# Low parts of the last six rows of W_out: two Pool operations in the place of one VectorE operation

## The chip, the core and the metric

The kernel runs on one core of a Trainium2 chip. The core has five engines, each with an instruction queue of its own that is worked off in order: TensorE (PE in the profile; PEld is its weight load), VectorE (DVE), ScalarE (ACT), GpSimd (POOL) and SyncE (SP, which here issues every DMA). The metric is the device time of one execution in microseconds; less is better.

## What is computed

One layer of a hybrid decoder. The input is normalised and projected, three groups of heads (a linear recurrence, a dilated-window attention and a state-space group, "SSD") make 2048 mixed columns, and these go through one output projection:

```python
mix = jnp.concatenate([y_lru, y_attn, y_ssd], axis=-1) @ w_out
out = x + rmsnorm(mix, post_g)
```

`w_out` is 2048 x 1024. The prompt has 2048 tokens. The products keep float32 accuracy: each operand is split into a high part in the rounded type fp32r and a low part, the difference, and three products of the four are summed.

## The kernel before

The program is written with a tile framework that sets the order of the instructions on each engine when the program is built. It takes the author's order as a guide and places an instruction where it reckons its operands to be ready, so a change of engine in one line moves neighbours too. On the chip the order is then fixed.

The stages are: projection (to about 1,110 us), sample tokens, prompt attention (to about 1,420 us), and a last stage in which two things run interleaved. One is the SSD group, 16 chunks of 128 tokens, each in two halves `g`; in it DVE, ACT and Pool make decay matrices (`sg`), scaled inputs (`xdt`, `xte`), the state (`hT`) and a group norm (`sq`, `rs`, `rB`), and PE makes the products `yd`, `yo` and `stp`. The other is `out_chunk`, the output projection: for each chunk of 128 tokens two output halves (`hf`, 512 columns each, tile `ops`), each a sum over 16 rows k of `W_out` blocks of three matmuls (`mm3`, lines 82 to 84: high by high, high by low, low by high). Rows 0 to 7 take `mh` and `ml`, the two other groups' output; rows 8 to 15 take `sh` and `sl`, the SSD group's. `ops` tiles lie in a pool of three.

`W_out` comes in just ahead of its first use. Rows 0 to 9 (`load_wo_slab`) are loaded whole in the attention stage. Rows 10 to 15 (`load_wo_rest`) are loaded in halves of 512 columns into a tile `wr` under the tag "x" that has two buffers, one for each half. For each half line 1001 makes the high part on ACT (`wo10h` to `wo15h`) and line 1002 the low part on DVE (`wo10l` to `wo15l`). Line 1002 is the last reader of `wr`; the DMA of the same half of the next row (line 1018) waits for it. The rows' scale is 1 for k below 8, and a column of the group-norm weight (`ngc`) for the others.

So the rows 10 to 15 go round a loop: DMA into `wr`, high part, low part, DMA of the next row. It lies in the first chunk of `out_chunk`, from about 1,436 to 1,465 us. Beside it the order puts matmuls of chunk 1's first output half.

Of the kernel before, what the change touches and what calls it, by code (L numbers as in the profile page):

```python
# [8 lines left out]
F32 = mybir.dt.float32  # L9
F32R = mybir.dt.float32r  # L10
AF = mybir.ActivationFunctionType
OP = mybir.AluOpType
# [15 lines left out]
W_SLAB = 10  # L28
# [4 lines left out]
def tile_hybrid_step(ctx: ExitStack, tc: tile.TileContext, A):  # L33
    nc = tc.nc
    act, dve, pool, pe, sp = nc.scalar, nc.vector, nc.gpsimd, nc.tensor, nc.sync
# [84 lines left out]
    def big(name, n=1024, dt=F32R):  # L120

        if n > 1024:
            return slab.tile([128, n], dt, tag="C", name=name, bufs=8)
        return slab.tile([128, n], dt, tag="A", name=name)
# [320 lines left out]
    with tc.tile_pool(name="dtp", bufs=1) as dp:  # L445
# [6 lines left out]
                                 op0=OP.mult, op1=OP.mult)  # L452
# [542 lines left out]
    wo = {}  # L995

    def load_wo(k, raw):
        wo[k] = [big(f"wo{k}{c}", 1024 if k < 12 else XC)[:, :DM] for c in "hl"]
        sc_ = 1.0 if k < 8 else ngc[:, k - 8:k - 7]
        for r, sl in raw:  # L1000
            act.activation(out=wo[k][0][:, sl], in_=r, func=AF.Copy, scale=sc_)
            dve.scalar_tensor_tensor(out=wo[k][1][:, sl], in0=r, scalar=sc_, in1=wo[k][0][:, sl].bitcast(F32),
                                     op0=OP.mult, op1=OP.subtract)

    def load_wo_slab():
        for k in range(W_SLAB):
            raw = big("wraw", dt=F32)
            sp.dma_start(out=raw, in_=A["w_out"][0, 128 * k:128 * k + 128])
            yield
            load_wo(k, [(raw, slice(0, DM))])  # L1010
            yield

    def load_wo_rest(pl):
        for k in range(W_SLAB, 16):
            raw = []
            for sl in (slice(0, 512), slice(512, DM)):
                raw.append((pl.tile([128, 512], F32, tag="x", name="wr", bufs=2), sl))
                sp.dma_start(out=raw[-1][0], in_=A["w_out"][0, 128 * k:128 * k + 128, sl])
            load_wo(k, raw)
            yield  # L1020
# [501 lines left out]
    for c in range(16):  # L1522
        k = 0
# [115 lines left out]
```

## Time and profile before

| | us |
|---|---|
| median of three runs | 1939.15 (1937.5 to 1939.77) |
| profiled execution, its own time | 1935.46 |
| its span in the trace | 1933.7 |
| PE busy in the span | 1888.0 (98%) |
| DVE busy | 1075.8 (56%) |
| ACT busy | 760.3 (39%) |
| POOL busy | 269.4 (14%) |

The profile is that of one execution. The span is what lies between its first and last instruction. Busy PE is modelled: a matmul's end is its result's arrival, so consecutive matmuls overlap in the rows, and an idle time before a matmul is the stretch in which none was under way.

### The profile page before, as it was taken

To read this page: it belongs to the slowest core of one execution; us is meant where nothing else is said; L and a number is where in the kernel's file an instruction comes from. 1 tells how busy PE (TensorE), PEld (TensorE's weight loads), DVE (VectorE), ACT (ScalarE), POOL (GpSimd) and SP (SyncE) were. 2 spreads that over 40 slices of the span, in tenths; PEclk is the share of its full clock that TensorE was granted. 3 is DMA by queue.
4 is the path that set the end of the run, shared out by engine and by line. 5 is a ranking of instruction groups with operands and counts; after the bars stand their busy time and mean duration, and the time that the engine had idled before them with its cause. 6 is when DMAs were issued, how large, how long until landed. Compare 5 with 4: busy or idle time off the path is not lost.

```text
span 1933.7 us, 35729 instructions
## 1 busy us (share of the span) xinstructions
PE 1888.0 (98%) x14110; PEld 1552.6 (80%) x14110; DVE 1075.8 (56%) x2354; ACT 760.3 (39%) x1490; POOL 269.4 (14%) x346
## 2 busy tenths in 40 slices
PE   8999999999999999999999999999998999999998
PEld 7998888888888888887877777777766787677876
DVE  7414444454533776664422226666687776667774
ACT  6411636362610222223233436555654333333332
POOL 0100111101010111111000100000023223223231
PEclk9999999999999999998999999999999999999999
DMA  7422121232233222224477753343465444334442
GB/s 235 131 79 74 44 69 47 64 69 63 66 88 79 94 76 74 67 72 138 131 210 205 208 181 115 101 142 102 119 207 161 127 140 124 111 115 130 128 140 66
DMA packets 304500, 222.02 MB, mean 115 GB/s; under 512 B 69171, under 2 KB 260515, under 8 KB 304333
## 3 DMA queue, kind: packets, MB, share of 16 engines
q1 hardware_dynamic: 304332, 219.74, 38.7%
q8 instruction: 111, 1.82, 0.4%
q14 instruction: 57, 0.46, 0.1%
HBM read 150.81 MB, written 68.86 MB: 114 GB/s over the span
## 4 chain that ended last, share of the span: by engine, by line
PE 41%; ACT 4%; DMA 3%; DVE 3%; issue 1%; SPq 1%; POOL 1%; DVEq 0%; ACTq 0%; POOLq 0%
PE ops L83 5%; PE ops L84 5%; PE ops L82 5%; PE mm L82 3%; PE pt L1164 3%; PE mm L84 3%; PE mm L83 3%; PE o L1200 2%; ACT sr L1136 2%; PE s L1109 2%; PE yd L1283 2%; DMA sg<-d_cum 1%; PE yo L1288 1%; PE s L1088 1%; PE stp L1307 1%
## 5 line engine op out<-in xcount | busy, mean ns | idle before, releaser
L82 PE MATMUL mm<-xh,wh 128*128 128x512 f32 (+2 forms) x1600 | 562.4, 351 | 1.8 <-ACT wh L147 0.9
L83 PE MATMUL mm<-xl,wh 128*128 128x512 f32 (+2 forms) x1600 | 561.2, 351 | 0.0
L84 PE MATMUL mm<-xh,wl 128*128 128x512 f32 (+2 forms) x1600 | 559.9, 350 | 0.0
L82 PEld LDWEIGHTS mm<-xh,wh 128*128 128x128 f32 x1600 | 301.5, 188 | 44.4 <-issue 4.3
L84 PEld LDWEIGHTS mm<-xh,wl 128*128 128x128 f32 x1600 | 300.6, 188 | 39.6 <-issue 1.0
L83 PEld LDWEIGHTS mm<-xl,wh 128*128 128x128 f32 x1600 | 301.2, 188 | 37.7 <-issue 0.2
L146 POOL TENSOR_TENSOR wr<-wr,gC 128x1024 f32<-128x1024 f32 x40 | 78.7, 1968 | 407.6 <-DMA wr<-in_w_in_dram 379.5
L436 DVE SCALAR_TENSOR_TENSOR o<-u,ssdc,o 128x512 f32<-128x512 f32 (+2 forms) x216 | 128.6, 618 | 4.8
L1136 ACT ACTIVATE sr<-sr,nm 128x384 f32<-128x384 f32 (+3 forms) x128 | 97.9, 770 | 23.3 <-DVE nm L1132 18.7
L148 DVE SCALAR_TENSOR_TENSOR wl<-wr,wh 128x1024 fp32r<-128x1024 f32 x40 | 48.9, 1223 | 82.9 <-ACT wh L147 82.9
L642 ACT ACTIVATE o<-o 128x512 f32<-128x512 f32 (+2 forms) x60 | 33.1, 552 | 145.7 <-issue 83.2
L1047 ACT COPY ptsb<-pt 128x512 f32<-128x512 f32 x96 | 52.5, 583 | 76.7 <-PE pt L1164 76.6
L720 DVE TENSOR_SCALAR sg<-sg,cum 128x128 f32<-128x128 f32 (+1 forms) x256 | 72.8, 344 | 14.7 <-ACT ecB L718 14.6
L82 PE MATMUL mmt<-wh,xh 128*128 128x256 f32 (+3 forms) x272 | 79.5, 295 | 0.9 <-ACT xh L254 0.6
L84 PE MATMUL mmt<-wh,xl 128*128 128x256 f32 (+3 forms) x272 | 78.6, 290 | 0.0
L83 PE MATMUL mmt<-wl,xh 128*128 128x256 f32 (+3 forms) x272 | 78.1, 288 | 0.0
L434 DVE TENSOR_SCALAR o<-u,ssdc 128x512 f32<-128x512 f32 (+1 forms) x72 | 43.1, 611 | 61.9 <-ACT u L416 60.7
L1164 PE MATMUL pt<-ident,sr 128*128 128x128 f32 x576 | 75.3, 281 | 2.3 <-ACT sr L1136 1.8
L147 ACT ACTIVATE wh<-wr 128x1024 fp32r<-128x1024 f32 x40 | 42.4, 1060 | 87.9 <-PE mm L83 76.9
L1164 PEld LDWEIGHTS pt<-ident,sr 128*128 128x128 f32 x576 | 63.6, 143 | 15.0 <-issue 8.9
L416 ACT COPY u<-mm 128x512 f32<-128x512 f32 (+1 forms) x80 | 39.4, 493 | 91.9 <-PE mm L84 80.2
L718 ACT ACTIVATE ecB<-sg 64x512 f32<-64x512 f32 x60 | 37.8, 630 | 88.3 <-DMA sg<-d_cum 80.5
(520 smaller groups left out, 3551.3 us busy)
## 6 DMA issues: line engine op xcount, KB each, us to landing
wr<-in_w_in_dram SPq DMA_DIRECT2D x40, 512.0 KB
sg<-d_cum SPq DMA_DIRECT2D x30, 512.0 KB
d_xbc<-o SPq DMA_DIRECT2D x36, 256.0 KB
x<-in_x_prompt_dram SPq DMA_DIRECT2D x32, 256.0 KB
kc<-in_cache_attn_k_dram SPq DMA_DIRECT2D x32, 256.0 KB
vt<-in_cache_attn_v_dram SPq DMA_DIRECT2D x32, 256.0 KB
xres<-in_x_prompt_dram SPq DMA_DIRECT2D x32, 256.0 KB
out_dram<-ot SPq DMA_DIRECT2D x32, 256.0 KB
```

What stands on the lines that cost most here:

```text
L82: pe.matmul(out, lhsT=wh, rhs=xh, start=start, stop=False)
L83: pe.matmul(out, lhsT=wh, rhs=xl, start=False, stop=False)
L84: pe.matmul(out, lhsT=wl, rhs=xh, start=False, stop=stop)
L146: pool.tensor_tensor(out=wr, in0=wr, in1=gC[:, :, None].to_broadcast([128, 8, 128]), op=OP.mult)
L147: act.activation(out=wh, in_=wr, func=AF.Copy, scale=scale)
L148: dve.scalar_tensor_tensor(out=wl, in0=wr, scalar=scale, in1=wh.bitcast(F32), op0=OP.mult, op1=OP.subtract)
L434: dve.tensor_scalar(out=o, in0=v(0), scalar1=w[:, 0:1], scalar2=b, op0=OP.mult, op1=OP.add)
L436: dve.scalar_tensor_tensor(out=o, in0=v(t), scalar=w[:, t:t + 1], in1=o, op0=OP.mult, op1=OP.add)
L720: dve.tensor_scalar(out=sg[:n, h], in0=sg[:n, h], scalar1=cum[:n, c, 8 * g + h:8 * g + h + 1], scalar2=0.0, op0=OP.subtract, op1=OP.min)
L1047: act.copy(out=out, in_=in_)
L1136: act.activation(out=sr[e][r], in_=sr[e][r], func=AF.Exp, bias=nm[:, e, r:r + 1], accum_out=ll[:, e, r:r + 1])
L1164: pe.transpose(tp[:, r], sr[e][r][:, 128 * g:128 * g + 128], ident)
```

## The change

For rows 10 to 15 of `W_out` the low part is no longer made by DVE in one operation (multiply by the scale, subtract the high part). Pool makes it in two: it scales `wr` in place, and then subtracts the high part from it. Rows 0 to 9 stay as they were. Twelve DVE operations go and 24 Pool operations come; all lines behind the edit have numbers that are higher by four.

```diff
         for r, sl in raw:
             act.activation(out=wo[k][0][:, sl], in_=r, func=AF.Copy, scale=sc_)
+            if k >= W_SLAB:
+                pool.tensor_scalar(out=r, in0=r, scalar1=sc_, scalar2=None, op0=OP.mult)
+                pool.tensor_tensor(out=wo[k][1][:, sl], in0=r, in1=wo[k][0][:, sl].bitcast(F32), op=OP.subtract)
+                continue
             dve.scalar_tensor_tensor(out=wo[k][1][:, sl], in0=r, scalar=sc_, in1=wo[k][0][:, sl].bitcast(F32),
                                      op0=OP.mult, op1=OP.subtract)
```

Pool before, from the first SSD chunk that runs beside the loop on: only the SSD steps stand there.

```order
L1277 TENSOR_TENSOR xb<-xb,dF 128x512
L742 TENSOR_TENSOR xte<-xdt,tend 128x512
L1312 TENSOR_TENSOR hT<-hT,dec 128x512
L1277 TENSOR_TENSOR xb<-xb,dF 128x512
L750 TENSOR_TENSOR sq<-sq 128x256
```

Pool now, rows 13 to 15 of the same loop, with the next half chunk's SSD steps among them.

```order
L1003 TENSOR_SCALAR wr<-wr,ngc 128x512
L1316 TENSOR_TENSOR hT<-hT,dec 128x512
L1004 TENSOR_TENSOR wo13l<-wr,wo13h 128x512
L1003 TENSOR_SCALAR wr<-wr,ngc 128x512
L1004 TENSOR_TENSOR wo14l<-wr,wo14h 128x512
L1003 TENSOR_SCALAR wr<-wr,ngc 128x512
L1004 TENSOR_TENSOR wo14l<-wr,wo14h 128x512
L1281 TENSOR_TENSOR xb<-xb,dF 128x512
L1003 TENSOR_SCALAR wr<-wr,ngc 128x512
L742 TENSOR_TENSOR xte<-xdt,tend 128x512
L1004 TENSOR_TENSOR wo15l<-wr,wo15h 128x512
```

The two operations of a half no longer stand together: a step of the SSD group can lie between them. From the first low part of row 10 to the last of row 15 nine SSD steps stand in Pool's queue (three `xte`, two `hT`, two `xb`, two `sq`).

PE before, where the last row of `W_out` is used (`wo0` to `wo9` with `mh`, `ml` are chunk 1's first output half, `wo15` is chunk 0's):

```order
L82 MATMUL ops<-wo15h,sh 128x512
L82 MATMUL ops<-wo5h,mh 128x512
L83 MATMUL ops<-wo5l,mh 128x512
L83 MATMUL ops<-wo15l,sh 128x512
L84 MATMUL ops<-wo15h,sl 128x512
L82 MATMUL ops<-wo15h,sh 128x512
L84 MATMUL ops<-wo5h,ml 128x512
L82 MATMUL ops<-wo6h,mh 128x512
L83 MATMUL ops<-wo15l,sh 128x512
```

PE now, at the same place, up to the first matmul of chunk 1's second output half (`wo0h`):

```order
L83 MATMUL ops<-wo15l,sh 128x512
L84 MATMUL ops<-wo15h,sl 128x512
L84 MATMUL ops<-wo10h,sl 128x512
L82 MATMUL ops<-wo11h,sh 128x512
L83 MATMUL ops<-wo15l,sh 128x512
L84 MATMUL ops<-wo15h,sl 128x512
L83 MATMUL ops<-wo11l,sh 128x512
L84 MATMUL ops<-wo11h,sl 128x512
L733 MATMUL tpx<-ident,xb 128x128 x4
L82 MATMUL ops<-wo0h,mh 128x512
```

The last use of row 15 has moved behind 15 more matmuls of chunk 1's first half (34 stand ahead of it, 19 before) and the transposes `tpx`. Between it and `wo0h` there are now three matmuls and one set of transposes; before, there were twelve matmuls and two sets of transposes (`tpb`, `tpx`).

## Rows read from the trace of the kernel before

**Rows 1.** Stretch; us; busy PE, PEld, DVE, ACT, POOL; clock; DMA share; GB/s.

```profile
1439.30:1470.30 31.00, 26.67 (x138) 18.22 (x137) 26.49 (x49) 16.65 (x30) 9.33 (x8) 1.00 0.58 179
...
1550.00:1900.00 350.00, 349.04 (x1986) 270.35 (x1985) 242.10 (x471) 128.07 (x267) 101.62 (x116) 1.00 0.42 125
```

**Rows 2.** Waits of SP's DMA queue, 1435 to 1470: us, times, longest.

```profile
SPq L1018 <- DVE wo14l L1002: 4.0, 2, 3.8
```

**Rows 3.** Line 1002, ns min/median/max, first and last start.

```profile
L1002 DVE SCALAR_TENSOR_TENSOR wo10l<-wr,ngc,wo10h x2: 747/1138/1530, 1436.7 to 1437.4; 128x512 fp32r<-128x512 f32 x2
```

**Rows 4.** DVE in order of time: start, us, instruction.

```profile
1436.75 2.19 DVE L1002 SCALAR_TENSOR_TENSOR wo10l<-wr,ngc,wo10h 128x512 fp32r<-128x512 f32 x2
...
1463.08 0.75 DVE L1002 SCALAR_TENSOR_TENSOR wo15l<-wr,ngc,wo15h 128x512 fp32r<-128x512 f32 x1
...
1464.34 0.74 DVE L1002 SCALAR_TENSOR_TENSOR wo15l<-wr,ngc,wo15h 128x512 fp32r<-128x512 f32 x1
```

**Rows 5.** POOL by line and shape over the whole span: busy us, mean ns.

```profile
L1312 POOL TENSOR_TENSOR hT<-hT,dec 128x512 f32<-128x512 f32 x30 | 31.3, 1044 | 40.1 <-PE yo L1288 39.6 <-ACT wo12h L1001 0.5
L750 POOL TENSOR_TENSOR sq<-sq 128x256 f32<-128x256 f32 x30 | 22.7, 755 | 87.4 <-ACT sq L749 87.4
L751 POOL TENSOR_TENSOR sq<-sq 128x128 f32<-128x128 f32 x30 | 14.8, 495 | 2.4
...
L1141 POOL COPY lb<-ll 128x512 f32<-128x512 f32 x16 | 9.8, 614 | 283.3 <-DVE ll L1139 210.6 <-DMA vn<-d_v 50.2 <-PE s L1109 22.5
```

**Rows 6.** POOL in order of time, beside the loop.

```profile
1436.81 1.58 POOL L1277 TENSOR_TENSOR xb<-xb,dF 128x512 f32<-128x512 f32 x1 [9.39 <-PE tpx L733]
1443.02 2.02 POOL L742 TENSOR_TENSOR xte<-xdt,tend 128x512 f32<-128x512 f32 x1 [4.63 <-DVE xdt L736]
...
1456.75 1.95 POOL L742 TENSOR_TENSOR xte<-xdt,tend 128x512 f32<-128x512 f32 x1 [2.70 <-DVE xdt L736]
```

**Rows 7.** ACT in order of time.

```profile
1435.58 1.33 ACT L1001 ACTIVATE wo10h<-wr,ngc 128x512 fp32r<-128x512 f32 x2
...
1462.09 0.72 ACT L1001 ACTIVATE wo15h<-wr,ngc 128x512 fp32r<-128x512 f32 x1 [3.99 <-DMA wr<-in_w_out_dram]
...
1467.50 0.60 ACT L1486 ACTIVATE jk<-ops 128x512 f32<-128x512 f32 x1
1468.11 0.20 ACT L1486 ACTIVATION_READ_ACCUMULATOR jk<-ops 128x1 f32 x1
...
1468.54 0.29 ACT L113 ACTIVATE rstd<-oss,eps_t 128x1 f32<-128x1 f32 x1
1468.86 0.20 ACT L114 ACTIVATE rstd<-rstd 128x1 f32<-128x1 f32 x1
```

**Rows 8.** DVE in order of time, end of chunk 0.

```profile
1468.34 0.16 DVE L1489 TENSOR_TENSOR oss<-oss 128x1 f32<-128x1 f32 x1 [0.16 <-ACT jk L1486]
...
1469.46 1.40 DVE L1500 SCALAR_TENSOR_TENSOR ot<-ops,rstd,pgB 128x512 f32<-128x512 f32 x2
```

**Rows 9.** PE in order of time; in brackets the idle time before, and its releaser.

```profile
1467.13 0.41 PE L701 MATMUL tpb<-ident,bc 128*128 128x128 f32 x2 [0.79 <-DMA bc<-d_xbc]
...
1468.62 0.66 PE L733 MATMUL tpx<-ident,xb 128*128 128x128 f32 x4
1469.04 0.48 PE L83 MATMUL ops<-wo8l,sh 128*128 128x512 f32 x1
...
1470.05 0.40 PE L84 MATMUL ops<-wo9h,sl 128*128 128x512 f32 x1
1470.28 0.48 PE L82 MATMUL ops<-wo0h,mh 128*128 128x512 f32 x1
...
1472.27 0.49 PE L754 MATMUL rs<-sq,ones 128*128 128x128 f32 x2 [0.82 <-POOL sq L751]
...
1485.00 0.49 PE L754 MATMUL rs<-sq,ones 128*128 128x128 f32 x2 [1.00 <-POOL sq L751]
...
1490.57 1.09 PE L1283 MATMUL yd<-sg,xdt 128*64 128x128 f32 x16 [0.48 <-DVE xdt L736]
```

## The prediction

> **What bounds the kernel now.** I read the busy times by stretch first. From 1,550 to 1,900 us PE is busy for 349.04 of 350.00 us at the full clock [rows 1]: the output stage runs at PE's pace, and what is lost or won ahead of it is neither given back nor added to there. The stretch in which the twelve edited operations lie, 1,439.3 to 1,470.3 us, is different: PE is busy for 26.67 of 31.00 us, so 4.33 us are idle, with DVE at 26.49 us and POOL at 9.33 us [rows 1]. After it, up to 1,492.5 us, PE waits three more times: 0.82, 1.00 and 0.48 us [rows 9]. From there on the instruction order is the same but for two single places. So the change can move the time only through these 53 us, and it can win at most 4.33 + 2.30 = 6.6 us, 0.34%. No such cap stands over a loss.
>
> Then I read who waits for the low parts. SP's queue waits for them, up to 3.8 us at once, 4.0 us for the two halves of row 14 alone [rows 2], and ACT then waits 3.99 us for the next `wr` [rows 7]. The loop DMA, high part, low part, DMA is what sets when row 15 arrives, so the latency of a low part counts, and not only who makes it.
>
> **What is removed.** Twelve DVE operations. Alone one takes 0.747 us, beside a Pool operation up to 1.530 us [rows 3]. That frees 9 to 11 us of DVE in a stretch in which DVE has 4.5 us idle. The SSD steps on DVE move forward by it, `xdt` above all. It shortens PE's waits only where PE waits for such a step, and the cap of 6.6 us holds for all of them together.
>
> **What is added.** Twelve scalings and twelve subtractions of 128 x 512 on Pool. The subtraction has the shape of `hT`: 1.044 us [rows 5]. A scaling on Pool is not in this trace. From below it is bounded by the copy of the same size, 0.614 us, which reads and writes as much and computes nothing; from above by the two-input operation, 1.044 us [rows 5]. I take 0.65, since it has one tensor input as the copy has. A low part then costs 0.65 + 1.04 = 1.69 us in place of 0.74, that is 0.95 more, or 1.35 with the upper price. Twelve of them are 20.3 us; with the 9.33 us that Pool has [rows 1] it is busy for 29.6 of 31 us. So Pool goes from idle to full, and what stands in its queue waits.
>
> **When row 15 is ready.** I follow one half through the loop.
> - Start. ACT ends the first high part of row 10 at 1435.58 + 0.72 = 1436.30 [rows 7]. On DVE the low part ended at 1436.75 + 0.75 = 1437.50 [rows 3, 4]. On Pool the scaling, then an `xb` that the order puts between, then the subtraction end at 1436.30 + 0.65 + 1.04 + 1.04 = 1439.03: 1.5 us later.
> - Five turns, to row 15: each is longer by 0.95, so 4.75 us. DMA and high part are taken as they are.
> - The second half: its low part ended 1465.08 - 1463.83 = 1.25 us behind the first [rows 4]; on Pool it is 1.69 behind, 0.44 more.
> - That is 6.7 us if nothing else stood in Pool's way. But nine SSD steps stand among the 24: three `xte`, two `hT` and two `xb` at 1.04, `sq` at 0.755 and 0.495 [rows 5], 8.5 us in all. Where Pool is waiting for a `wr` they cost nothing, elsewhere all. I take half, 4.3 us, since with Pool at 29.6 of 31 us they can't all slot in, while each half's loop leaves Pool waiting for a DMA once a turn.
>
> So the last low part is ready 11.0 us later (6.7 to 15.2), at about 1,476 us.
>
> **What PE does meanwhile.** The new order puts 15 more matmuls of chunk 1 and a set of transposes ahead of the last use of row 15. A matmul issues every 0.23 us (1470.05 to 1470.28), the transposes take 0.42 (1468.62 to 1469.04) [rows 9]: 3.9 us of cover, at no cost, as the work is only moved. What they hide is gone behind it. Chunk 1's second half (`wo0h`) needs an `ops` buffer that chunk 0 frees at its end: the last matmul 0.39, ACT 0.60 + 0.20, DVE 0.16, ACT 0.29 + 0.20, DVE's `ot` 0.70 [rows 7, 8], 2.5 us. Before, twelve matmuls lay over that and `wo0h` started with no wait [rows 9]; now three matmuls and one set of transposes do, 1.1 us. PE waits 1.4 us that it did not wait before.
>
> **What comes back.** Once row 15 is in, PE had four more waits: 0.79, 0.82, 1.00 and 0.48 us, all for the SSD group's steps and loads [rows 9]. These steps don't hang on row 15; when PE comes late they are done. I give all of it back, 3.1 us. The steps on Pool among them (`sq`) stand behind the last low part in its queue, so this is the generous end.
>
> **Sum.** 11.0 - 3.9 + 1.4 - 3.1 = +5.4 us: 1940.9 for the profiled execution (1935.46), and 1944.5 against the median of 1939.15. With no SSD step in the way it is +1.1, with all of them +9.6, and with scaling at the upper price 6 x 0.4 = 2.4 more, +12.0.
>
> **A rule on the shared port.** The row shows it first: the second `wo10l` took 1.530 us in place of 0.747 while Pool's `xb` ran, and that `xb` took 1.58 in place of 1.04; two `xte` took 2.02 and 1.95 [rows 3, 6]. The two engines hold each other up. The Trainium skill, "SBUF — State Buffer", section "SBUF: two separate sides", says that a DVE operation with two SBUF inputs and a GpSimd operation exclude each other for a whole instruction, and the trace agrees. It speaks against this change, and is the third rival below.
>
> **The rivals.**
> 1. Pool has time enough: the SSD steps slot into Pool's waits for DMA, the loop is 6.7 us longer, and cover and later waits take nearly all of it: +1.1 us, 1940.3. For it: Pool's SSD steps have slack before (`xb` came after 9.39 us of idle [rows 6]). Against: half of them feed PE directly. It decides if less than 2.7 us of the 8.5 lie in the loop.
> 2. Faster. DVE's relief decides: with nothing of the loop on it, DVE has `xdt` and `sg` ready sooner, and PE's waits up to 1,492.5 us vanish. All of them are worth -6.6 us (1932.5), half of them -3.3. It needs low parts that are ready no later than now. Against it: 1.69 us with an empty queue is more than the 0.74 of DVE, and DVE's own queue ahead of a low part would have to be longer than Pool's by 0.95 us in every turn. Only rows whose DVE operation was held up to 1.53 come near that.
> 3. Port. The three of Pool's eight operations in the stretch that were held up were so by 0.54, 0.98 and 0.91 us over 1.04 [rows 6], 2.4 us or 0.3 for each of the eight. With two operations a turn and six turns, the loop grows by 3.6 us more: +9.0, 1948.2.
> 4. The change isn't made: excluded, since the order of the new program has the 24 operations on Pool and none of the twelve on DVE.
>
> **How the numbers follow.** About 0.2%, 3.9 us, is what a measurement here can tell from no change. The forecast (+4 to +8) has 0.40, the third rival and the upper price (+8 to +12) 0.15, the first rival 0.35, the second 0.10. The first rival lies within 0.2%. The forecast lies above it, and so does the third: slower 0.55, same 0.36, faster 0.09, as a part of the second is too small to be told. The range leaves out most of the second rival and the far end of the third with the upper price: 1937.0 to 1950.0.
>
> **What would show it.** In the new trace the low parts on lines 1003 and 1004 should be near 0.65 and 1.04 us, with single ones held up by half a microsecond or more; the last low part of row 15 should end near 1,476 us, counted from the same start; Pool should be over 85% busy from 1,437 to 1,470; PE should wait by name for Pool's `wo..l`, and once for `ot` at chunk 1's second half; and the idle of PE from there to 1,492 should be smaller than 2.3 us. Wrong it would be if the scaling costs far from 0.6 to 1.04, if the last low part is ready by 1,472, or if PE's later waits stay in full though it comes late.

## The result and the profile after

| | before | after |
|---|---|---|
| median of three runs, us | 1939.15 (1937.5 to 1939.77) | 1957.92 (1957.16 to 1958.4) |
| profiled execution, us | 1935.46 | 1957.92 |
| span in the trace, us | 1933.7 | 1956.1 |
| POOL busy, us | 269.4 | 306.6 |

The change costs 18.8 us by the two medians. The ratio is 1.011, with an interval of 1.0094 to 1.0126, which is 18.2 to 24.4 us, 21.3 in the middle; the two profiled executions differ by 22.5. In the comparisons further down the kernel before has medians of 1937.05 to 1937.45 us, some 2 us less than in this one. So what a run below gives back of the loss is read against about 21 us and not against 18.8. The forecast was +5.4, with a range from -2 to +11: the direction was right, the size was not.

The first view is Pool in order of time, after (start, us, instruction; in brackets the idle time before it).

```profile
1435.20 1.86 POOL L1003 TENSOR_SCALAR wr<-wr,ngc 128x512 f32<-128x512 f32 x1 [8.46 <-ACT wo10h L1001]
1437.04 2.04 POOL L1281 TENSOR_TENSOR xb<-xb,dF 128x512 f32<-128x512 f32 x1
1439.04 1.72 POOL L1004 TENSOR_TENSOR wo10l<-wr,wo10h 128x512 fp32r<-128x512 f32 x1
1440.74 2.52 POOL L1003 TENSOR_SCALAR wr<-wr,ngc 128x512 f32<-128x512 f32 x1
...
1463.29 1.56 POOL L1003 TENSOR_SCALAR wr<-wr,ngc 128x512 f32<-128x512 f32 x1 [1.30 <-ACT wo13h L1001]
...
1466.17 1.56 POOL L1003 TENSOR_SCALAR wr<-wr,ngc 128x512 f32<-128x512 f32 x1
1468.25 1.04 POOL L1316 TENSOR_TENSOR hT<-hT,dec 128x512 f32<-128x512 f32 x1 [0.51 <-PE yo L1292]
1469.25 1.27 POOL L1004 TENSOR_TENSOR wo13l<-wr,wo13h 128x512 fp32r<-128x512 f32 x1
1472.73 1.75 POOL L1003 TENSOR_SCALAR wr<-wr,ngc 128x512 f32<-128x512 f32 x1 [2.21 <-ACT wo14h L1001]
...
1480.73 1.04 POOL L1281 TENSOR_TENSOR xb<-xb,dF 128x512 f32<-128x512 f32 x1 [2.02 <-PE tpx L733]
...
1487.16 1.26 POOL L1004 TENSOR_TENSOR wo15l<-wr,wo15h 128x512 fp32r<-128x512 f32 x1
```

Undisturbed, the scaling takes 1.56 us and the subtraction 1.26 us: 2.82 us for a low part, where 1.69 was reckoned. The bracketed idle times tell the rest: between 1435.20 and 1463.29, where Pool waits 1.30 us for a high part, no row has one. Behind that there are three more (0.51, 2.21 and 2.02 us), so that Pool is idle for 6.0 of the 53.2 us up to the end of the last low part. The last low part of row 15 ends at 1488.42. To compare places in two traces I count from the last `rs` matmul ahead of `wo6h` (PE, 1435.39 before, 1434.26 after): the last low part lay 29.7 us behind it before [rows 4], and lies 54.2 us behind it now, 24.5 us later.

The second view is PE's waits after, from that `rs` to the first `ops<-wo12h,sl` behind `yo`, where the two orders have come together again (engine line, what it waited for: us, times, longest).

```profile
PE ops L83 <- POOL wo15l L1004: 4.3, 2, 2.6
PE rs L754 <- POOL sq L751: 4.0, 2, 2.7
PE ops L83 <- POOL wo14l L1004: 2.8, 2, 1.7
PE stp L1311 <- POOL xte L742: 2.8, 1, 2.8
PE ops L83 <- POOL wo11l L1004: 2.5, 1, 2.5
PE ops L82 <- DVE ot L1504: 0.7, 1, 0.7
```

PE waits by name for `wo..l` and once for `ot`, as the prediction had it. But two kinds of work are waited for, and both are Pool's: low parts, and the SSD steps `sq` and `xte` that stand between them in its queue. The third view is the busy times of that whole stretch, first of before, then of after (stretch; us; busy PE, PEld, DVE, ACT, POOL; granted clock; DMA share; GB/s).

```profile
1435.39:1492.51 57.12, 50.49 (x277) 36.99 (x277) 46.92 (x81) 27.46 (x52) 18.07 (x17) 1.00 0.52 157
```

```profile
1434.26:1513.98 79.72, 61.43 (x277) 43.76 (x277) 41.72 (x68) 27.85 (x51) 52.48 (x41) 0.83 0.37 110
...
1445.00:1455.00 10.00, 7.50 (x21) 4.94 (x20) 6.68 (x12) 3.33 (x5) 9.80 (x8) 0.57 0.52 169
...
1475.00:1485.00 10.00, 5.38 (x24) 3.89 (x24) 0.69 (x1) 1.82 (x3) 7.90 (x7) 1.00 0.18 52
1485.00:1495.00 10.00, 7.05 (x19) 5.05 (x20) 3.85 (x6) 2.50 (x7) 5.43 (x6) 0.64 0.38 122
...
1550.00:1900.00 350.00, 347.90 (x1969) 269.56 (x1968) 243.74 (x473) 128.29 (x267) 101.19 (x114) 1.00 0.42 126
```

The same 277 matmuls took 57.12 us and now take 79.72: 22.6 us more, which is all that the two profiled executions differ by (22.5). From 1,550 us on nothing has changed [rows 1]. PE's idle time in the stretch went from 6.6 to 18.3 us (stretch less busy), and its busy time from 50.5 to 61.4 for the same matmuls. The growth of the busy time goes with the clock: 1.00 before, 0.83 now, and 0.57 in one stretch of 10 us. The fourth view shows how it comes, PE in order of time after a wait.

```profile
1449.32 0.80 PE L83 MATMUL ops<-wo11l,sh 128*128 128x512 f32 x1 [2.50 <-POOL wo11l L1004]
1449.91 0.63 PE L84 MATMUL ops<-wo11h,sl 128*128 128x512 f32 x1
1450.34 0.63 PE L82 MATMUL ops<-wo8h,sh 128*128 128x512 f32 x1
1450.76 0.63 PE L83 MATMUL ops<-wo8l,sh 128*128 128x512 f32 x1
```

Behind an idle time of 2.50 us the matmuls start 0.42 to 0.43 us apart, at the lower of the two levels (1.2 GHz), where [rows 9] have 0.23 at the upper (2.4 GHz). Does the clock cost time of its own, or does it only fill time in which PE would have waited anyway? For the part of the stretch that lies behind the last use of row 15's low part the trace gives an estimate, since PE waits there for 2.0 us in all (1.33 for `sq`, 0.67 for `ot`; before, 3.1). First before, then after:

```profile
1465.16:1492.51 27.35, 24.11 (x139) 18.14 (x138) 20.33 (x39) 11.61 (x25) 8.10 (x9) 1.00 0.51 161
```

```profile
1488.48:1513.98 25.50, 23.49 (x116) 18.02 (x117) 17.00 (x29) 8.92 (x19) 5.92 (x7) 0.81 0.37 114
```

At the busy time of before, 116 matmuls would take 24.11 x 116 / 139 = 20.1 us; they take 23.5. That is 3.4 us for the lower clock, an estimate, and the wait for `ot` may hide one of them. For the 7.5 us of added busy time that lie ahead of this place the trace doesn't settle it; an experiment asks it too.

### The profile page after: what moved, and what is told of

The parts are those of the page before. It is cut to its first block, busy times and chain, and to the rows that moved or that the text cites. A ratio compares the mean times of both kernels' runs of the same rounds, so it can differ in the third digit from the quotient of the medians.

```text
span 1956.1 us, 35749 instructions
## 1 busy us (share of the span) xinstructions
PE 1900.7 (97%) x14110; PEld 1559.9 (80%) x14110; DVE 1072.3 (55%) x2342; ACT 761.0 (39%) x1490; POOL 306.6 (16%) x370
## 4 chain that ended last, share of the span: by engine, by line
PE 43%; ACT 3%; DVE 2%; DMA 2%; POOL 2%; issue 2%; SPq 0%; DVEq 0%; ACTq 0%; POOLq 0%
PE ops L82 5%; PE ops L84 5%; PE ops L83 5%; PE pt L1168 3%; PE mm L82 3%; PE mm L84 3%; PE mm L83 3%; PE o L1204 2%; PE s L1113 2%; ACT sr L1140 2%; PE yd L1287 2%; PE s L1092 1%; PE yo L1292 1%; PE stp L1311 1%; PE tp L903 1%
## 5 line engine op out<-in xcount | busy, mean ns | idle before, releaser
L1168 PEld LDWEIGHTS pt<-ident,sr 128*128 128x128 f32 x576 | 65.1, 145 | 15.2 <-issue 9.1
```

The costliest lines, as they stand in the source:

```text
L1168: pe.transpose(tp[:, r], sr[e][r][:, 128 * g:128 * g + 128], ident)
```

## The experiments

The names in brackets are those of the runs. My first theory was that the loop's latency makes the loss, as the prediction had it, with wrong prices. The rivals were Pool's queue (what stands behind the new operations), the port that Pool and DVE share, and the clock. Ratios are to the kernel before, run on the same chip in turn with each kernel; 0.1% are 1.9 us.

**The prices** (prices). At the program's start, ahead of Pool's first work of any length, nine kinds of operation three times each on scratch tiles:

```diff
+        for _ in range(3):
+            pool.tensor_scalar(out=po, in0=pa, scalar1=eps_t[:, 0:1], ...)
+            pool.tensor_scalar(out=po, in0=pa, scalar1=1.25, ...)
+            ...
```

> The kernel before, with 27 extra Pool operations on 128x512 scratch tiles at the very start, where no work of the kernel waits for them for long: scaling with a per-partition scalar, the same with a constant, the same in place, copies and subtractions with float32 and fp32r output, a product with a broadcast operand. Theory (price of the two operations): in the changed kernel's trace the scaling took 1.56 us and the subtraction into fp32r 1.26 us with nothing beside them; here the per-partition scaling should again be 1.5 to 1.6, the float32 subtraction 1.04 and the fp32r one 1.26. If the price comes from the per-partition scalar, the scaling by a constant is near the copy's 0.61; if it is the operation itself, it is 1.5 too. Rival (port): alone, the scaling is 0.6 to 1.04 and the subtraction 1.04, and what the changed kernel showed was VectorE in the way.

Pool by line and shape (busy us, mean ns | idle before):

```profile
L208 POOL TENSOR_SCALAR po<-pa,eps_t 128x512 f32<-128x512 f32 x3 | 4.7, 1564 | 0.3
L210 POOL TENSOR_SCALAR pa<-pa,eps_t 128x512 f32<-128x512 f32 x3 | 4.7, 1562 | 0.3
L209 POOL TENSOR_SCALAR po<-pa 128x512 f32<-128x512 f32 x3 | 4.5, 1489 | 0.2
L213 POOL TENSOR_TENSOR po<-pa,pc 128x512 f32<-128x512 f32 x3 | 3.8, 1262 | 0.0
...
L216 POOL TENSOR_TENSOR po<-pa,eps_t 128x512 f32<-128x512 f32 x3 | 3.1, 1038 | 0.2
...
L211 POOL COPY po<-pa 128x512 f32<-128x512 f32 x3 | 1.8, 609 | 0.2
```

So the prices in the changed kernel are the ordinary ones. 1.04 us is the price of a product whose second operand is broadcast (`hT`, `xb`, `xte` are all such); two full tensors cost 1.26, and a scaling by a scalar, with one tensor input, is the dearest of all. (This program ran once, in 1975.13 us, and its time isn't used.)

**No low parts at all for rows 10 to 15** (nolow), the most that the change could have won:

```diff
+            if k >= W_SLAB:
+                continue
             dve.scalar_tensor_tensor(out=wo[k][1][:, sl], ...
```

> The kernel before with no low parts made for rows 10 to 15 at all: their products take the low part of row 0, so these rows' products are not those of the reference. It shows what the twelve VectorE operations cost the kernel before, so what the change could win at best. Both theories: between -1 and -6.6 us, the cap that the idle time of TensorE sets; I expect -3.

1934.32 us, ratio 0.9984 (0.9975 to 0.9993): 3.0 us were to be had. The prediction's cap of 6.6 us was right as a cap.

**The subtraction alone on Pool** (subonly; 1.26 us a half, and the rows' scale is left out):

```diff
-                pool.tensor_scalar(out=r, in0=r, scalar1=sc_, scalar2=None, op0=OP.mult)
                 pool.tensor_tensor(out=wo[k][1][:, sl], in0=r, in1=wo[k][0][:, sl].bitcast(F32), op=OP.subtract)
```

> The changed kernel without the scaling of rows 10 to 15: the high part is made without scale and Pool only subtracts, one operation of 1.26 us for each half. The norm's scale of these rows is left out of the computation. Theory (latency): a low part costs 1.26 us in place of 0.74, a turn is 0.5 longer, five turns 2.6 us, Pool has 15 us more instead of 34; +1 to +6 us against the kernel before. Rival (each Pool operation in the way costs, by the port): half of the operations are left, +8 to +11 us.

1943.45 us, ratio 1.0037 (1.0024 to 1.0051): +6.2, just above the theory's range and well below the rival's.

**The scaling as a broadcast product** (ttscale; 1.04 us in place of 1.56; the order stays as in the changed kernel):

```diff
-                pool.tensor_scalar(out=r, in0=r, scalar1=sc_, scalar2=None, op0=OP.mult)
+                pool.tensor_tensor(out=r, in0=r, in1=sc_.to_broadcast([128, 512]), op=OP.mult)
```

> The changed kernel with Pool's scaling written as a product of two tensors, the second one the scale broadcast over the row: by the run with single prices 1.04 us in place of 1.56. Everything else as in the changed kernel. Theory (Pool's queue is full, its length sets the time): 12 x 0.52 = 6.2 us less in Pool's queue, so +9 to +14 us against the kernel before in place of +18.8. Rival (port: each Pool operation that reads two tensors holds VectorE up): as many operations with two inputs and more, +16 to +20 us.

1954.24 us, ratio 1.0085 (1.0071 to 1.0099): +17.0, which lies in the rival's range. But both ranges were reckoned from +18.8. Every engine but Pool has the same instructions in the same order as in the changed kernel, so the stretch can be set beside that of the third view:

```profile
1437.16:1509.32 72.16, 57.26 (x277) 41.67 (x277) 47.71 (x69) 28.18 (x52) 48.07 (x41) 0.88 0.40 121
```

It is 15.0 us longer than before, where the changed kernel's is 22.6 longer. So 6.2 us less on Pool gave 7.6 us back in the traces and 4.8 by the ratios; the 1.8 us by the medians come from the different medians of the kernel before. This speaks for the length of Pool's queue, and the number in the rival's range doesn't speak for the port.

**Low parts on DVE, the load on Pool** (load). The loop is as before, and PE's order too but for one matmul; Pool gets 24 operations of the same shapes, whose results nobody uses:

```diff
             dve.scalar_tensor_tensor(out=wo[k][1][:, sl], in0=r, scalar=sc_, ...)
+            if k >= W_SLAB:
+                pool.tensor_scalar(out=junk, in0=pgB[:, sl], scalar1=sc_, ...)
+                pool.tensor_tensor(out=junk..., in0=pgB[:, sl], in1=wo[k][0][:, sl]..., op=OP.subtract)
```

> Low parts on VectorE as before; the 24 Pool operations stand in the program as well, with the same shapes and the same wait for the high part, but they read a constant tile and write a scratch tile that nobody reads. So Pool's queue is as full and the port is as contended as in the changed kernel, only the loop of the rows doesn't hang on Pool. Theory (latency of the low part in the loop): the greater part of the 18.8 us is gone, +2 to +8 us against the kernel before, for the SSD steps that still queue behind. Rival (Pool's queue and the port): +12 to +19 us, as the changed kernel.

1955.35 us, ratio 1.0097 (1.0083 to 1.0111): +18.1. My theory fell here. Nothing in the rows' loop waits for Pool, and most of the loss is there. PE's waits:

```profile
PE rs L754 <- POOL sq L751: 7.4, 2, 6.4
PE ops L82 <- DVE ot L1504: 3.9, 1, 3.9
PE stp L1310 <- POOL xte L742: 3.6, 1, 3.6
```

**The same length of queue, hardly reading** (memload). In place of the 24 operations, 12 copies of one column and 60 memsets:

```diff
+                pool.tensor_copy(out=junk[:, 0:1], in_=wo[k][0][:, sl][:, 0:1]...)
+                for _ in range(5):
+                    pool.memset(junk, 0.5)
```

> As the run with the full Pool queue beside low parts on VectorE, but the Pool operations read next to nothing: for each half one column of the high part is copied (so that it waits as the others did) and a scratch tile is set to a constant five times, 5 x 0.5 us. Pool's queue is about as long, 12 x 2.6 to 2.8 us. Theory (queue: the SSD steps stand behind): +10 to +18 us against the kernel before. Rival (port, through the reading of tensors): 0 to +5 us, and no VectorE operation that is held up.

1945.63 us, ratio 1.0035 (1.0023 to 1.0048): +8.4, between the two expectations. Pool was busy for 57.1 us from 1,436 to 1,516, and for 56.1 in the run before. The difference is seen in DVE's low parts, two rows of each (line 1002, ns min/median/max), first with tensors read on Pool, then with memsets:

```profile
L1002 DVE SCALAR_TENSOR_TENSOR wo10l<-wr,ngc,wo10h x2: 1524/1659/1794, 1438.0 to 1439.8; 128x512 fp32r<-128x512 f32 x2
...
L1002 DVE SCALAR_TENSOR_TENSOR wo14l<-wr,ngc,wo14h x2: 1534/1646/1759, 1471.5 to 1472.9; 128x512 fp32r<-128x512 f32 x2
```

```profile
L1002 DVE SCALAR_TENSOR_TENSOR wo10l<-wr,ngc,wo10h x2: 743/744/746, 1437.9 to 1438.5; 128x512 fp32r<-128x512 f32 x2
...
L1002 DVE SCALAR_TENSOR_TENSOR wo14l<-wr,ngc,wo14h x2: 739/740/740, 1463.7 to 1464.4; 128x512 fp32r<-128x512 f32 x2
```

An operation of 0.74 us takes up to 1.8 beside Pool operations that read tensors (the twelve lie between 0.74 and 1.79, six of them over 1.5), and 0.74 beside memsets (one of the twelve 0.96). The Trainium skill, "SBUF — State Buffer", section "SBUF: two separate sides", has it so: the lock between DVE and GpSimd counts, for a DVE operation with two SBUF inputs, only against a GpSimd operation that reads SBUF. The trace agrees; the prediction's sentence on that page lacks the condition. So of the 18.1 us about 8 are the queue and about 10 come with the reading. (PE's order differs between the two runs in a few places behind row 15.)

**The SSD steps of chunk 1 on DVE**, in the changed kernel (ssddve), in the one before (b_ssddve), and in the load run (load_ssddve). The edit is the same in all three:

```diff
-        pool.tensor_tensor(out=xte[:n], in0=xdt[:n], ...
+        (dve if c == 1 else pool).tensor_tensor(out=xte[:n], in0=xdt[:n], ...
...
-            norm = group_norm(ck, ps6, y, 128, dve if c == 0 else pool)
+            norm = group_norm(ck, ps6, y, 128, dve if c <= 1 else pool)
```

(and so for `xb` and `hT`).

> The changed kernel with Pool's SSD steps of chunk 1 (two xb, two xte, two hT, two pairs of sq) moved to VectorE, which has been freed of twelve operations. Low parts stay on Pool. Theory (SSD steps behind the low parts in Pool's queue are the greater part): +3 to +9 us against the kernel before. Rival (low parts that come late to TensorE are the greater part, whoever makes the SSD steps): +12 to +19 us.

> The kernel before (low parts on VectorE as they were), with the SSD steps of chunk 1 (xb, xte, hT, sq) moved from Pool to VectorE. It is the control for load_ssddve. VectorE gets some 9 us more in a stretch where it had 4.5 us idle, so 0 to +4 us against before; over +6 would say that VectorE can't carry them and that load_ssddve must be read against this run, not against before.

> The run load (low parts on VectorE, 24 operations of the same shapes on Pool on a scratch tile) with the SSD steps of chunk 1 moved to VectorE as well, so nothing that TensorE needs stands behind the 24 operations. Theory A (two paths through Pool's queue, the late low parts and the late SSD steps, and each alone is enough for the loss): with both gone the loss of 18.1 us of load falls to 0 to +5 us over b_ssddve, which is what the shared port still costs. Theory B (the port decides: Pool's operations slow VectorE's, whatever stands in Pool's queue): +9 to +16 us over b_ssddve.

The changed kernel so: 1955.0 us, 1.009 (1.0076 to 1.0104), +17.7: with the SSD steps gone from Pool the late low parts alone hold most of the loss, in an order of its own. The one before: 1.0023 (1.0012 to 1.0035), +4.5, just above the 0 to +4 that was expected; its twelve executions lie in two heaps, at 1936 to 1939 and at 1943 to 1946, so its median, 1943.76 (+6.7), tells less than the ratio. The load run: 1950.21 us, 1.0058 (1.0046 to 1.0071), +11.2, which is 6.8 over its control where load alone was +18.1. Most of the loss of load has gone with the steps in Pool's queue. What is left lies between the two theories (0 to 5, and 9 to 16): the port may well have a share, as the waits that are left name DVE's and ACT's work in the profiled execution, the fastest of the five. Here are PE's longest waits, first of the changed kernel with the edit, then of the load run with it:

```profile
PE ops L83 <- DMA sg<-d_cum: 3.5, 1, 3.5
PE ops L83 <- POOL wo13l L1004: 2.6, 2, 1.7
PE ops L82 <- DVE ot L1504: 2.5, 1, 2.5
PE ops L83 <- POOL wo15l L1004: 2.2, 2, 2.0
```

```profile
PE ops L82 <- ACT wo14h L1001: 2.8, 2, 2.3
PE rs L754 <- DVE sq L751: 2.2, 2, 1.4
PE ops L83 <- DVE wo11l L1002: 1.5, 1, 1.5
```

The first row names a DMA for a matmul whose operand is Pool's `wo11l`; I read it as Pool's: that low part ends at 1449.52, and the matmul starts at 1449.57.

**A third buffer for `wr`** (and for the two other tiles under the tag "x"), in the changed kernel (bufs3) and in the one before (b_bufs3):

```diff
-                raw.append((pl.tile([128, 512], F32, tag="x", name="wr", bufs=2), sl))
+                raw.append((pl.tile([128, 512], F32, tag="x", name="wr", bufs=3), sl))
```

> The changed kernel with three wr buffers in place of two, so that the DMA of a half no longer waits for the low part just ahead of it. Theory A (Pool is overfull, 43 us of work in a stretch of 31): the buffers don't help, +15 to +19 us. Theory B (the latency of DMA, high part, low part round the loop sets the time, as the prediction reckoned it): a third buffer takes a third of the loop away, +4 to +11 us.

> The kernel before with three wr buffers in place of two: it looks for a version that beats both. Before, ScalarE waited 4 us for a wr and TensorE was idle for some 6.8 us in this place. If the wait for a free buffer is what sets those waits: -1 to -3 us. If the order that the scheduler makes of it or the SSD steps set them: -0.5 to +2 us.

1954.11 us, 1.0083 (1.0066 to 1.01), for the changed kernel: a loop with half more room gives 4 to 5 us of some 21 back, in an order of its own and with executions from 1948.04 to 1958.58. Theory A's range held, so its round trip is not the main thing that sets the pace. The kernel before becomes 1935.43 us, 0.9988 (0.9978 to 0.9997): 1.6 to 2.3 us faster than it was, and the fastest version with the whole computation. It is less than the 0.2% that the prediction counts as a difference.

**Work for PE in the waits** (fill). 40 matmuls with a zero operand (9.2 us at 0.23) ahead of the low-part products of rows 11 to 15, in the changed kernel, to keep the clock up:

```diff
+                for _ in range(4):
+                    pe.matmul(ps[:n], lhsT=zero, rhs=wo[0][0][:, sl], start=False, stop=False)
```

> The changed kernel with four more matmuls by a tile of zeros ahead of the low-part product of rows 11 to 15 in chunk 0 (ten times four, 0.23 us each at the full clock, 9.2 us if nothing hides them). They add nothing to the sum and keep TensorE at work in its waits. In the changed kernel's trace the granted clock is 0.57 to 0.92 in the stretch after the waits. Theory (the lower clock after the waits costs 8 to 10 of the 18.8 us): the clock stays higher and the time falls, +9 to +15 us against the kernel before. Rival (the waits are all, the clock costs nothing of its own): +18 to +24 us.

1960.27 us, 1.0113 (1.0098 to 1.0129), +23.0. The granted clock from 1,436 to 1,516 us rose from 0.83 to 0.91, and the time did not fall: 9.2 us of work were added, and the ratio is the changed kernel's (1.011) to within the noise. The rival's range held. It is no clean test, as the longest two waits of its trace (`stp` 2.8, `rs` 3.4) have no filler ahead of them and the order is not the changed kernel's, so the clock's own share stays unsettled where PE also waits for Pool.

**The price that the prediction had, in the changed kernel's order** (predprice). A copy in place (0.61) and a subtraction against a broadcast column (1.04) make 1.65 us. PE, DVE, ACT and SP have the same instructions in the same order as in the changed kernel, and Pool the same places:

```diff
-                pool.tensor_scalar(out=r, in0=r, scalar1=sc_, scalar2=None, op0=OP.mult)
-                pool.tensor_tensor(out=wo[k][1][:, sl], in0=r, in1=wo[k][0][:, sl].bitcast(F32), op=OP.subtract)
+                pool.tensor_copy(out=r, in_=r)
+                pool.tensor_tensor(out=wo[k][1][:, sl], in0=r, in1=ngc[:, k - 8:k - 7].to_broadcast([128, 512]), op=OP.subtract)
```

> The changed kernel with its order kept instruction by instruction on every engine, but each scaling replaced by a copy in place (0.61 us) and each subtraction by one against a broadcast column (1.04 us): 1.65 us a half, the price that the prediction reckoned with, in place of 2.82. The low parts of rows 10 to 15 are wrong numbers. Theory A (the price of the two operations is the step that failed, the rest of the sum holds): +3 to +8 us, near the +5.4 that was forecast. Theory B (the price is a part only, and the step that lets half of the SSD steps slot into Pool's waits failed too): +9 to +13 us.

1947.82 us, ratio 1.0053 (1.0036 to 1.007): +10.4. But the six executions lie in two heaps: three at 1944.07 to 1944.85, +6.6 to +7.4 and in theory A's range, and three at 1950.79 to 1952.77, +13.3 to +15.3 and above B's. The median lies between them, and the interval (+7.0 to +13.6) shuts out neither theory. The trace is of the slowest, 1952.77. Its last low part and its stretch:

```profile
1483.40 1.04 POOL L1004 TENSOR_TENSOR wo15l<-wr,ngc 128x512 fp32r<-128x512 f32 x1
...
1439.18:1508.40 69.22, 58.57 (x277) 41.64 (x277) 42.26 (x69) 27.89 (x51) 39.38 (x41) 0.88 0.42 127
```

The low part ends 45.3 us behind `rs`, 15.6 later than before. At its own price the prediction said 11.0, and 15.2 if every SSD step counts. The stretch is 12.1 us longer than before, in B's range; the `rs` itself starts 3.8 us later (1439.18 against 1435.39), a delay from ahead of the stretch. So this execution speaks for B, and of the lower heap there is no trace.

**Pool as cheap as DVE** (cheap). A copy of one column (0.19) and one of 128 x 512 (0.62), 0.8 us a half:

```diff
+                pool.tensor_copy(out=r[:, 0:1], in_=r[:, 0:1])
+                pool.tensor_copy(out=wo[k][1][:, sl], in_=r)
```

> The changed kernel with low parts that cost Pool what one costs VectorE: a copy of one column in place and a copy of 128 x 512 into the low part, 0.7 us a half. The low parts of rows 10 to 15 are wrong numbers. Theory A (Pool's time decides: 8.5 us of low parts and 9.3 us of SSD steps fit into the stretch): -2 to +3 us. Theory B (the move itself, its new order and Pool's queue, costs at any price): +5 to +10 us.

1937.62 us, ratio 1.0003 (0.9995 to 1.0012): no difference. At this price the move costs nothing that can be told, and the relief of DVE brings nothing by itself. The order is one of its own, though (PE's matmuls differ from the changed kernel's order in 34 places), so what the changed kernel's order costs at such a price no run shows.

**Rows 13 to 15 alone on Pool** (from13):

```diff
-            if k >= W_SLAB:
+            if k >= 13:
```

> The change for rows 13 to 15 alone: 6 halves, 16.9 us of Pool time in place of 33.8, and rows 10 to 12 on VectorE. Theory A (what counts is by how much Pool's work exceeds the stretch it stands in; some 17 + 5 us in 15 us): +8 to +14 us. Theory B (the loss goes with the number of rows): +9.4 us or less, +5 to +9.5.

1950.79 us, ratio 1.0066 (1.0053 to 1.0079): +13.3, in theory A's range. Half of the rows make 60 to 70% of the loss, so it doesn't go with their number. That it goes with how far Pool is overfull where the operations stand fits, but is not shown by this run alone, as its order is its own too.

Side by side, the runs with all low parts of rows 10 to 15 on Pool. The last two columns are from the traces and count from `rs` as above; the lower three kernels have the same order on every engine but Pool, where only the operations differ.

| kernel | Pool us for a half | time against before | last low part later by | stretch longer by |
|---|---|---|---|---|
| cheap (own order) | 0.80 | +0.2 | 2.9 | |
| predprice | 1.65 | +10.4 | 15.6 | 12.1 |
| ttscale | 2.30 | +17.0 | 17.9 | 15.0 |
| changed kernel | 2.82 | +18.8 (by the ratio +21.3) | 24.5 | 22.6 |

## Why the prediction was wrong in its size

**What bounds the kernel now: right.** All of the loss lies in the one stretch that was named, and nothing behind 1,550 us moved. The cap on a gain held (3.0 us of 6.6).

**What is removed: right.** Cheap shows that the relief of DVE is worth nothing that can be told, as the low chance of the second rival had it.

**What is added: this step failed.** The scaling was given 0.65 us, bounded by the copy and by a two-input operation. It takes 1.56, outside of both bounds, which the prediction had named as a sign that it is wrong. A low part costs Pool 2.82 us and not 1.69. The Trainium skill, "GPSIMD Engine Reference", section "4.1 Engine selection", says that a one-input elementwise operation runs on GpSimd at roughly line rate and a two-input one about twice as slowly as on VectorE. The trace agrees on the copy (0.61), and on two inputs (1.26 against 0.68 us for VectorE's `sl`); for the scaling it doesn't, and the measurement decides. The subtraction was given `hT`'s 1.04 because its shape was the same. But `hT`'s second operand is a broadcast column block, and the subtraction's is a full tensor. [rows 5] had two operations of that kind, the `sq` sums: 0.495 us for 128 columns and 0.755 for 256, so 0.26 more for each 128, which gives 0.755 + 2 x 0.26 = 1.275 for 512. It takes 1.26. This number was there to be read, and the wrong row was taken. Predprice sizes the whole error of price: in the same order the loss is 1.0053 in place of 1.011, 11 us less by the ratios, and the stretch is 10.5 us shorter in the traces.

**When row 15 is ready: mis-sized too, in its parts.** "I take half" of the 8.5 us of SSD steps, because they slot into Pool's waits for a `wr`. In the changed kernel Pool waits for a high part only twice more after the first, 1.30 and 2.21 us, 3.5 in all. Two more waits (0.51 and 2.02 us) are of another kind, which the sum had at nothing: an SSD step waits for PE (`hT` for `yo`, `xb` for `tpx`), and all that stands behind it in the queue waits too. In the trace of predprice, at the predicted price, Pool does wait for a high part in four of the five turns, 6.3 us in all, as the prediction said. The last low part is 15.6 us late even so: the SSD steps waited for PE for 4.1 us (2.10 and 2.02), and the operations were held up by some 5 us over their undisturbed prices. So it is luck that 15.6 is near the 15.2 with all SSD steps, as far as this one trace shows.

With right prices and all SSD steps the prediction's own sum reads: start +2.7, five turns 5 x 2.08 = 10.4, second half +1.6, SSD steps 8.5, together 23.2, where 24.5 was measured. With cover 3.9, the `ot` wait 1.4 and 3.1 given back it gives +17.6. The profiled executions, from which all of its terms are read, differ by 22.5, so the nearness to the 18.8 of the medians proves nothing. What is missing can be named: 1.3 us of the last low part, 1.3 that did not come back, and about 3 for the lower clock behind it, less 0.7 of the `ot` wait. That is a sum made afterwards.

**What the sum doesn't show.** It has one path, the rows' loop. The runs show two: in load no low part waits for Pool, in ssddve no SSD step of chunk 1 does, and each keeps most of the loss (1.0097 and 1.009 of 1.011). So removing one of them gives little back. In load about half of it comes with Pool's reading of tensors, as memload shows, and not with the queue alone.

**What PE does meanwhile, and what comes back: too generous.** Together these terms were to take 5.6 us off the 11.0. In the profiled executions they take 1.9 off the 24.5. The wait for `ot` was 0.7 us in place of 1.4, as PE went more slowly meanwhile. Of the later waits (0.79, 0.82, 1.00, 0.48) one for `sq` (1.00) stayed and grew to 1.33, as the prediction's own remark on the "generous end" allows, so 1.8 of the 3.1 us came back. The remaining 3 us are about what the lower clock costs there.

**The port rival: right in the size of its term, partly by luck.** It expected 3.6 us; one of the three delays that it averaged over the eight operations of the stretch is that of the `xb` at 1436.81, which lies ahead of it, so its own rows give 2.8. In the changed kernel the 24 operations and the three `xb` are 3.6 us over their undisturbed prices (scalings 20.7 - 12 x 1.56 = 2.0, subtractions 0.5, `xb` 4.2 - 3 x 1.04 = 1.1). It costs far more where DVE has two-input work left on the path, as load shows.

**The clock had no term.** In the stretch PE's busy time grew by 10.9 us for the same matmuls. About 3 of them lie behind the last low part, where hardly a wait could hide them. Ahead of it fill raised the clock and gained nothing, so it seems that much of the rest fills time in which PE would have waited for Pool. That is an inference, and no run settles it.

## What to carry to other kernels

Price an operation by a row of the same kind of operands, not of the same shape: full tensor, broadcast column and scalar are three prices on Pool, and an operation that no row shows has no upper bound in one that has more inputs. When the work added fills an idle engine (here 33.8 + 9.3 us in a stretch of 31), count everything that stands in its queue as late, unless the trace shows waits long enough to take it, and ask what each step in that queue itself waits for. Look for who else hangs on it, since a second path nearly as long as the first makes a single remedy look nearly useless. And compare two changed kernels by the same stretch of their traces when they have the same order, as here the median of the kernel before moved by 2 us between comparisons.

## What the runs showed of the hardware

- On Pool, a tensor times a per-partition scalar (1.56 us for 128 x 512, run prices) is dearer than the product with the same scalar broadcast as a second operand (1.04), and than the difference of two full tensors (1.26). A scaling by a constant takes 1.49, and in place or not makes no difference (1.56). For the copy and the subtraction the output type fp32r makes none either (0.61, 1.26).
- Beside Pool's memsets a two-input DVE operation stays at 0.74 us (memload; one of twelve 0.96); beside Pool operations that read tensors it takes up to 1.8 (load).
- Behind waits of 2.5 to 2.8 us PE's matmuls went on at the lower clock level: 0.57 granted on average from 1,445 to 1,455 us, and 0.83 over the 79.7 us that hold the waits. Behind the last low part 116 matmuls took 23.5 us at 0.81, where 139 had taken 24.1 at 1.00.
